# Full rows and columns for the score, gate-bias and Fourier-fold products of a two-layer hybrid backbone

## The chip, the cores and the metric

The kernel runs on one core of a Trainium2 chip. The metric is the device time of one execution in microseconds (us), the median over runs. The engines named below are TensorE (PE; its weight loads are PEld), VectorE (DVE), ScalarE (ACT), GpSimd (POOL) and SyncE (SP), which issues most DMAs.

## The reference, cut to what matters

Two layers work on 640 tokens (128 of a prompt, 512 latent ones) of width 1024. Each layer has a mixer of three branches and a gated FFN. What the change touches:

```
f = fft2(u, axes=(tokens, channels of a group of 128)).real        # branch A, 4 groups
z = (a_lr @ w_a2) + b_a                                             # branch B, gate logits, two directions
log_a = log_sigmoid(z) / 16
s = (q @ k.T) / 8;  p = softmax(s)                                  # branch C, 4 heads x 2 maps, 64 features
o = (p[map 0] - lam * p[map 1]) @ v
```

Prompt tokens see 128 keys, latent tokens 640 (128 of a cache and 512 latent ones).

## The kernel before, in words

All weight products run with operands split in a high and a low part of fp32r, three products for one (high by high, high by low, low by high; lines 391 to 393). A unit of weights is loaded, split by ScalarE (line 362) and GpSimd (line 366), and used for 640 tokens in two parts, 384 and 256 columns. TensorE runs the instructions in the order in which the program writes them. Between two groups of weight products comes a step of the other work: `slot` counts columns and calls `step`, which advances the first generator in a queue. VectorE, ScalarE and GpSimd are put in order by the scheduler, except in stretches that are written out.

**Attention (branch C).** For each layer two pairs of heads; a pair is ten tiles of 128 queries (two heads, one context tile and four latent ones each), so 40 tiles in the program, 32 of them latent. `attention` is a pipeline with ten stages, one step for each: `queries` transposes the queries of a tile into a bank of PSUM and makes their high part (ScalarE, line 1050) and their low part (GpSimd, line 1053); two steps later `maps` makes the scores; two steps after that `turn` transposes the weights, then `mix` multiplies them with the values. The 64 features of a key stand twice on the 128 partitions: in one half is the high part, in the other the low part. So the product of the high queries, whose 64 features also stand twice, takes 128 rows and yields high by high plus high by low (line 1068). The product of the low queries with the high keys takes 64 rows, the upper or lower ones for the two maps (line 1069). A latent tile has two maps of two halves of 320 keys: eight products, four of either kind in turn. A context tile has four, of 128 keys. The scores of a map take one of two PSUM buffers named `big`, which the maximum (line 1076) and the exponential (line 1079) read.

**Gates (branch B).** `gla` adds two products for each of five token tiles (line 735): the activations `aT` with 128 rows, and `ones`, 64 rows, with a table whose rows 0 and 32 hold the high and the low part of the bias. It runs once for each of two head pairs in a layer, so there are four such stretches of ten products.

**Fourier (branch A).** `fourier` takes four groups in each layer. The latent tokens are folded at their middle, which leaves one token over: its column of 128 channels is multiplied as a stationary operand with one column (line 686), and the row that results is added with a product of one row (line 709). Both are plain fp32 products, which TensorE issues twice.

**Modulation.** In layer 0 VectorE also computes the modulation (line 577), a step after so many columns of products.

Of the kernel before, what the change touches and what calls it, by code (L numbers as in the profile page):

```python
# [12 lines left out]
F32 = mybir.dt.float32  # L13
# [18 lines left out]
# the tokens in two parts, one ahead of the other  # L32
SPLIT = (slice(0, 384), slice(384, T))
STILES = ((0, 1, 2), (3, 4))
# (feature tile, part): of the last ones, the first part all before the other
# [4 lines left out]
# tiles of [128, 640]; columns of products between two steps of other work  # L40
# [6 lines left out]
def _fm(w, cols):  # L47
    """[K, M] columns as [128, K/128, 128]: one tile of output features."""
    k = w.shape[0] // P
    return w[:, cols].reshape(k, P, P).transpose(1, 0, 2)  # L50
# [66 lines left out]
def pack_mod(w):  # L117
    """The first 2048 columns of [1024, 6144] as [128, 512]: 256 of the shift and of the scale, one k tile."""
    return w[:, :2048].reshape(KT, P, 2, 4, 256).transpose(3, 0, 1, 2, 4).reshape(32, P, 512)


def pack_modt(w):
    """The columns on the partitions, as [128, 512]: 128 columns, half of the rows."""
    return w.T.reshape(48, P, 2, 512).transpose(0, 2, 1, 3).reshape(96, P, 512)


# [1 line left out]
def constants():  # L128
# [44 lines left out]
    # keys of a chunk, queries of the same half  # L173
# [8 lines left out]
# small parameters of a layer, in one [128, S] array  # L182
S_N1, S_N2, S_BM, S_GLA, S_DIF = 0, 8, 16, 64, 192
S_SIZE = 192 + 128
# and those of the differential attention
# [25 lines left out]
def pack_a2(i, l):  # L211
    """[128, 4, 128]: rows the two directions' low-rank gates, four times; [64, 4, 128]: the bias in row 0 and row 32;
    (pair, direction) columns."""
    w = i["w_gla_a2"][l]
    a, b = np.zeros((P, 4, P), w.dtype), np.zeros((64, 4, P), w.dtype)
    for pr in range(2):
        for d in range(2):
            s = slice(pr * P, pr * P + P)
            for r in range(d * 16, P, 32):
                a[r : r + 16, pr * 2 + d] = w[d][:, s]  # L220
            b[::32, pr * 2 + d] = i["b_gla_a"][l][d, s]
    return np.concatenate([a, b])


def layout(i):
# [13 lines left out]
        # [layer, pair, 2 x 64, (head, map), keys]: the 64 features twice  # L239
# [9 lines left out]
class Kernel:  # L249
    """The products of the layers' weights run on TensorE group after group; between the groups, a step at a  # L250
    time, comes the work of the branches that hangs on other engines (`side`) and of the modulation (`back`)."""
# [20 lines left out]
    # -- allocation --  # L272
# [22 lines left out]
    # -- the order of the work --  # L295
    def slot(self, cols):
        """After a product group of so many columns: steps of the other work."""
# [29 lines left out]
    def pipe(self, n, *stages):  # L327
        """Steps: stage s on item i in step i + s, the later stages first; what a stage returns is called after all of them, and so on."""
# [7 lines left out]
    # -- weights --  # L336
    def load_weight(self, halves=False):
        """The next unit in the order of use, from DRAM."""
# [10 lines left out]
    def split_weight(self, late=False):  # L349
        """The next unit in two parts."""  # L350
# [25 lines left out]
    def used(self, l, u):  # L376
        """All products of a unit are issued: its place goes to a later one."""
        del self.ws[l * N_UNITS + u]
        self.split_weight()

    def split(self, src, h, lo, eng=None):
        """src = h + lo, both of few enough bits for one pass of TensorE."""
# [3 lines left out]
    def acc3(self, ps, pairs):  # L386
        """ps = sum of (wh + wl).T @ (xh + xl) over pairs, each part in one pass."""
# [7 lines left out]
    def group(self, w, k0, nk, act, s):  # L395
        """128 output features for a part of the tokens."""
# [6 lines left out]
    def begin(self, l, us):  # L403
        """The first tokens' products of several units side by side, as their activations come."""
# [9 lines left out]
    def units(self, l, us, act, ahead=0):  # L414
        """Yields (index, ps, tokens) of the feature units us; of the first ones, the first tokens all before the others."""
# [22 lines left out]
    def proj_tm(self, l, u, act):  # L438
        """256 columns, tokens on partitions: yields (ps, token tile)."""
# [24 lines left out]
    # -- small arithmetic --  # L464
    def rsqrt(self, v, n):
        """v ** -0.5 for [128, n] in SBUF."""
# [14 lines left out]
    def load_consts(self):  # L481
# [7 lines left out]
        # with columns of zeros, so that its products fill a quarter of the array  # L489
# [4 lines left out]
    def silu(self, c, t):  # L494
        """c = c * (1 + tanh(c / 2)) / 2"""
# [22 lines left out]
    # -- modulation --  # L518
# [7 lines left out]
    def mod_first(self, raws, c, small, mod, scale1):  # L526
        """Two tiles of the first layer's first shift and scale, for both conditions: products on TensorE. Yields after
        each k; the last step turns the features to the partitions."""
# [22 lines left out]
    def mod_next(self, l, m0, m1, small, mod):  # L551
        """The columns on the partitions, tiles m0 to m1 of 128: products and their sums on VectorE."""
# [31 lines left out]
    def mod_scale(self, mod, small, gain, tile0, name):  # L584
        """gain * (1 + scale): [128, 8, 2]."""
# [7 lines left out]
    # -- norms over the model dimension --  # L593
# [9 lines left out]
    def norm_diag(self, acc, tiles):  # L603
        """1 / rms of some of the tokens, as diagonals."""
# [17 lines left out]
    def norm_rows(self, dg, ps):  # L622
        """1 / rms on all partitions."""
# [29 lines left out]
    def modulate(self, xs, acc, scale, mod, shift0, p, out):  # L653
        """h = x * rstd * scale + shift for a part of the tokens, split in two parts."""
# [7 lines left out]
    # -- branch A --  # L662
    def folds(self, u):
        """Latent tokens t and TL - t folded, since the transform's cosines are even and its sines odd."""
# [9 lines left out]
    def fourier(self, tab, us, fold, out):  # L674
# [6 lines left out]
        def channels(g):  # L681
# [4 lines left out]
            nc.tensor.matmul(pc[0:1, 256:384], u[:, TC + n2 : TC + n2 + 1], cs[:, :P], start=True, stop=True)  # L686
# [5 lines left out]
            def end():  # L692
                nc.scalar.copy(zc[:, :256], pc[:, :256])
                nc.scalar.copy(zc[0:1, 256:384], pc[0:1, 256:384])
                nc.scalar.copy(z[:, :512], pz)
# [3 lines left out]
        def tokens(g):  # L699
# [9 lines left out]
            nc.tensor.matmul(pb[:, :258], zc[0:1, 256:384], self.c("nyq", tab["fou_c"])[0:1], start=False, stop=True)  # L709
# [13 lines left out]
    # -- branch B --  # L723
    def gla(self, l, pr, aT, a2, k, q, vs, rg, outs):
        """One pair of heads. k, q: [2 heads x 64, tokens]; vs[h], rg[h]: [token, token tile, 128]."""
        nc = self.nc
        c3 = lambda ap: ap.rearrange("p (c i) -> p c i", c=NT)
        # -log_sigmoid(z) = log(1 + exp(-|z|)) + max(-z, 0)
# [23 lines left out]
        # log decay from the chunk's start (or to its end), inclusive  # L752
# [10 lines left out]
        # [keys, head, token tile, queries of the same half]  # L763
# [3 lines left out]
        def scores(kk, qq, flip=0):  # L767
            """[keys, head, 5 x 64]: the queries of the keys' half of a tile (flip: of the other half)."""
# [10 lines left out]
        # the chunks' keys decayed to their ends, and the queries from their starts  # L779
        es, dls = [], []  # L780
        # the two directions of a head, one under the other
# [31 lines left out]
        def state(d):  # L813
# [16 lines left out]
            # the state that a tile of tokens finds  # L830
# [4 lines left out]
        # attention inside a chunk, by halves of blocks; both directions in one product  # L835
# [25 lines left out]
        def place(x, y, src, copy):  # L861
            """Scores of the keys' half x and the queries' half y, to where the products with v take them."""
# [38 lines left out]
    def head_norm(self, o, gain):  # L901
        """RMS norm over the 128 of [128 tokens, token tile, 128], times gain."""
# [14 lines left out]
    def head_out(self, on, out):  # L917
        """Features to the partitions, and split."""
# [8 lines left out]
    # -- branch C --  # L927
# [34 lines left out]
    def stack(self, m, src, out):  # L962
        """The parts of [64 features twice, n]: the high one under (m = 0) or over (m = 1) the low one."""
# [4 lines left out]
    def qk_prep(self, xs, tab, out, keys=None, ko=None):  # L968
        """xs[h]: [token, token tile, 2 x 64]: QK norm, rotary; the keys transposed, a map apart, in parts."""
# [14 lines left out]
        def rotate(h):  # L984
            # a map's features twice
# [5 lines left out]
            for m in range(2):  # L991
                x, ym, wm = m4(xn)[:, :, m], m4(y[m]), m4(w)[:, 1:, m]
                # context tokens carry no position
# [28 lines left out]
    def attention(self, pr, qy, kT, kx, vd, vc, nlam, gd, outs):  # L1022
        """A pair of heads. kT[(head, map)]: the cache's and the latent tokens' keys in parts; kx [2 x 64, (head, map) x
        keys]: the context tokens'; vc [keys, head x 128]: the cache's values."""
        nc = self.nc
        qs, ps_, ws, os_ = {}, {}, {}, {}
        # a bank of PSUM that the stages of a step share: queries, outputs, a tile of the weights
# [13 lines left out]
        def queries(i):  # L1041
# [5 lines left out]
            def end():  # L1047
                q, x = self.unit("q", F32R), self.sm([P, 256], "qf", 2)
                nc.scalar.copy(x, ps[:, :256])
                nc.scalar.copy(q[:, :256], x)  # L1050
                for m in range(2):
                    r, c = slice(64 * m, 64 * m + 64), slice(m * P, (m + 1) * P)
                    nc.gpsimd.tensor_sub(q[r, 256:384], x[r, c], q[r, c].bitcast(F32))
# [4 lines left out]
        def maps(i):  # L1058
# [4 lines left out]
            for m in range(2):  # L1063
                r = slice(64 * m, 64 * m + 64)
                S = self.big().rearrange("p (x n) -> p x n", x=2)[:, :parts, :n]
                for x in range(parts):
                    k = kx[:, (2 * j + m) * P : (2 * j + m + 1) * P] if t == 0 else kT[2 * j + m][:, x * n : (x + 1) * n]
                    nc.tensor.matmul(S[:, x], q[:, m * P : (m + 1) * P], k, start=True, stop=False)  # L1068
                    nc.tensor.matmul(S[:, x], q[r, 256:384], k[r], start=False, stop=True)  # L1069
# [71 lines left out]
    # -- merge --  # L1141
    def gate(self, l, u, h):
        """tanh(gate / 2), 128 features."""
# [5 lines left out]
    def merge(self, l, u, m, act, tg, merged, first=False, parts=None):  # L1149
        """merged += (1 + tanh(gate / 2)) * y, twice the gated branch."""  # L1150
# [26 lines left out]
    def residual(self, x, ps, s, g, m):  # L1177
        """x += g * ps for a part of the tokens (in place)."""
# [5 lines left out]
    # -- one layer --  # L1184
# [11 lines left out]
    def rgate(self, l, pr, h, small, rg):  # L1196
        """silu(r) * gain"""
# [11 lines left out]
    def mixer(self, l, h, small, backs):  # L1209
        nc = self.nc  # L1210
        # Fourier
# [13 lines left out]
        # GLA  # L1225
        # 32 columns, four times; the low part of the weights in the second place. Below, the places' rows are multiplied
        # by the parts of the next weights: high and high, low and high, high and low, and the rest of the first
# [263 lines left out]
```

## Time and profile before

| | |
|---|---|
| median of 3 runs | 2443.65 us (2440.45 to 2444.65) |
| span of the profiled execution | 2444.8 us |
| TensorE busy | 2337.2 us, 96% |
| weight loads busy | 2241.7 us, 92% |
| VectorE, ScalarE, GpSimd busy | 1412.1, 881.6, 958.3 us |
| granted TensorE clock, mean | 0.985 |

The profiled execution has no time of its own beside its span; the span lies 1.15 us above the median of the runs. The ends of matmuls in a profile are modelled: two products that follow each other overlap in it, so what one costs is the distance from its start to the next one's start. A product shows as rows*columns of the array, then partitions x columns of its moving operand.

### The profile page before, as it was taken

How to read it: one execution, taken by the hardware profiler on the slowest of the kernel's cores; microseconds unless marked ns; L12 is line 12 of the kernel's file. 1: busy time of each engine (PE TensorE's matmuls, PEld its weight loads, DVE VectorE, ACT ScalarE, POOL GpSimd, SP SyncE). 2: the span in 40 equal slices, each digit the busy share in tenths (PEclk: the TensorE clock that was granted, in tenths of full speed). 3: DMA queues.
4: the chain of work that ended last, by engine and by line, in shares of the span. 5: the costliest groups of instructions: out<-in, count | busy, mean ns of one | idle time of the engine just before them, and what ended most of it. 6: DMA issues, size and time to landing. Idle time of an engine off the chain costs nothing.

```text
span 2444.8 us, 42698 instructions
## 1 busy us (share of the span) xinstructions
PE 2337.2 (96%) x17060; PEld 2241.7 (92%) x17060; DVE 1412.1 (58%) x3062; ACT 881.6 (36%) x2016; POOL 958.3 (39%) x835
## 2 busy tenths in 40 slices
PE   6989999999998999999989999999999989999999
PEld 4888898989988999999979999989899989999999
DVE  5897785665866585886464657856642462122222
ACT  3444445444243321212234554454533332122221
POOL 1343543342433443434333445524423353333332
PEclk9999999999999999999999999999999999999999
DMA  7433211111611352443331222202113122222222
GB/s 279 149 118 97 83 64 48 57 53 45 238 63 44 134 182 95 155 150 135 104 106 59 80 72 73 72 31 66 53 52 121 53 70 77 78 72 76 78 73 74
DMA packets 90181, 227.99 MB, mean 93 GB/s; under 512 B 12416, under 2 KB 20480, under 8 KB 89984
## 3 DMA queue, kind: packets, MB, share of 16 engines
q1 hardware_dynamic: 85504, 218.69, 26.2%
q10 hardware_dynamic: 4480, 6.59, 0.8%
q8 instruction: 134, 2.20, 0.4%
q14 instruction: 63, 0.52, 0.1%
HBM read 213.70 MB, written 6.82 MB: 90 GB/s over the span
## 4 chain that ended last, share of the span: by engine, by line
PE 73%; DVE 17%; issue 3%; DMA 2%; POOL 2%; ACT 1%; ACTq 0%; SPq 0%; DVEq 0%; POOLq 0%
PE main L391 20%; PE main L392 20%; PE main L393 20%; DVE junk L577 4%; PE big L412 3%; PE big L1069 2%; DVE w L1000 2%; PE big L1068 2%; PE misc L1120 2%; PE big L776 1%; DMA rawm<-in_w_modt_dram 1%; DVE rs_t L472 1%; DVE ht L650 1%; PE misc L1100 1%; DVE tg L1159 1%
## 5 line engine op out<-in xcount | busy, mean ns | idle before, releaser
L366 POOL TENSOR_TENSOR wl<-raw,wh 128x512 fp32r<-128x512 f32 x552 | 759.0, 1395 | 1167.5 <-ACT wh L362 1071.8
L362 ACT CAST wh<-raw 128x512 fp32r<-128x512 f32 x556 | 329.4, 618 | 509.0 <-PE main L392 254.6
L391 PE MATMUL main<-h2h,wh 128*128 128x256 f32 (+1 forms) x1344 | 413.3, 308 | 0.8 <-DVE tt L1315 0.8
L393 PE MATMUL main<-h2h,wl 128*128 128x256 f32 (+1 forms) x1344 | 412.9, 307 | 0.0
L392 PE MATMUL main<-h2l,wh 128*128 128x256 f32 (+1 forms) x1344 | 412.8, 307 | 0.0
L577 DVE SCALAR_TENSOR_TENSOR junk<-rawm,cond 128x512 bf16<-128x512 f32 x320 | 287.6, 899 | 40.0 <-DMA rawm<-in_w_modt_dram 35.1
L391 PE MATMUL main<-hh,wh 128*128 128x384 f32 (+1 forms) x960 | 301.3, 314 | 5.2 <-DVE rx L1201 3.5
L393 PE MATMUL main<-hh,wl 128*128 128x384 f32 (+1 forms) x960 | 296.1, 308 | 0.0
L392 PE MATMUL main<-hl,wh 128*128 128x384 f32 (+1 forms) x960 | 295.9, 308 | 0.0
L391 PEld LDWEIGHTS main<-h2h,wh 128*128 128x128 f32 x1344 | 254.6, 189 | 1.7 <-DVE tt L1315 1.3
L392 PEld LDWEIGHTS main<-h2l,wh 128*128 128x128 f32 x1344 | 254.7, 190 | 0.0
L393 PEld LDWEIGHTS main<-h2h,wl 128*128 128x128 f32 x1344 | 254.6, 189 | 0.0
L391 PE MATMUL main<-wh,hh 128*128 128x256 f32 x800 | 237.3, 297 | 0.7 <-ACT tm L461 0.7
L392 PE MATMUL main<-wl,hh 128*128 128x256 f32 x800 | 230.8, 289 | 0.0
L393 PE MATMUL main<-wh,hl 128*128 128x256 f32 x800 | 230.7, 288 | 0.0
L391 PE MATMUL main<-ah,wh 128*128 128x384 f32 (+1 forms) x704 | 219.8, 312 | 10.2 <-DVE x L1182 9.5
L392 PE MATMUL main<-al,wh 128*128 128x384 f32 (+1 forms) x704 | 218.2, 310 | 0.0
L393 PE MATMUL main<-ah,wl 128*128 128x384 f32 (+1 forms) x704 | 218.0, 310 | 0.0
L1182 DVE SCALAR_TENSOR_TENSOR x<-main,g,x 128x256 f32<-128x256 f32 (+1 forms) x192 | 78.0, 435 | 210.1 <-PE main L393 210.1
L391 PEld LDWEIGHTS main<-hh,wh 128*128 128x128 f32 x960 | 183.2, 191 | 7.2 <-DVE rx L1201 3.7
L392 PEld LDWEIGHTS main<-hl,wh 128*128 128x128 f32 x960 | 183.5, 191 | 0.0
L393 PEld LDWEIGHTS main<-hh,wl 128*128 128x128 f32 x960 | 183.3, 191 | 0.0
(281 smaller groups left out, 4774.6 us busy)
## 6 DMA issues: line engine op xcount, KB each, us to landing
raw<-in_w_dram SPq DMA_DIRECT2D x276, 512.0 KB, 3.2
rawm<-in_w_modt_dram SPq DMA_DIRECT2D x160, 256.0 KB, 4.2
rawm<-in_w_mod_dram SPq DMA_DIRECT2D x32, 256.0 KB, 5.4
x<-in_x_t_dram SPq DMA_DIRECT2D x12, 320.0 KB, 6.3
cond<-in_cond_b_dram SPq DMA_DIRECT2D x12, 256.0 KB, 5.5
qds<-qd SPq DMA_DIRECT2D x16, 160.0 KB, 2.6
x<-xd SPq DMA_DIRECT2D x8, 320.0 KB, 5.2
states<-state SPq DMA_DIRECT2D x16, 128.0 KB, 3.6
```

The lines of the kernel that those rows point to most:

```text
L362: nc.scalar.copy(h[:, c], raw)
L366: (nc.vector if late else nc.gpsimd).tensor_sub(lo[:, c], raw, h[:, c].bitcast(F32))
L391: nc.tensor.matmul(ps, wh, xh, start=(i == 0), stop=False)
L392: nc.tensor.matmul(ps, wh, xl, start=False, stop=False)
L393: nc.tensor.matmul(ps, wl, xh, start=False, stop=(i == n - 1))
L412: self.nc.tensor.matmul(self.banks[i], a, b, start=(k == 0 and n == 0), stop=(k == KT - 1 and n == 2))
L577: nc.vector.scalar_tensor_tensor(self.sm([P, 512], "junk", 1, mybir.dt.bfloat16), raw, 1.0, cond[i, k], op0=ALU.mult, op1=ALU.mult, accum_ ...
L1000: nc.vector.tensor_mul(hv(wm)[:, :, a, b], hv(x[:, 1:])[:, :, a, 1 - b], hv(sn)[:, :, a, b])
L1068: nc.tensor.matmul(S[:, x], q[:, m * P : (m + 1) * P], k, start=True, stop=False)
L1069: nc.tensor.matmul(S[:, x], q[r, 256:384], k[r], start=False, stop=True)
L1120: nc.tensor.matmul(ps, wT[:, x * P : (x + 1) * P], v, start=(x == 0), stop=(x == n - 1))
L1182: nc.vector.scalar_tensor_tensor(x[:, r], ps[:, r.start - s.start : r.stop - s.start], g[:, m, i : i + 1], x[:, r], op0=ALU.mult, op1=ALU.add)
```

## The change

The low part of the queries is made by one subtraction over 128 partitions and both maps, and its product takes 128 rows, as that of the high part does (it now adds low by low as well). The ones and the bias table are extended to 128 rows, with zeros in the table. In the Fourier branch the token left over is multiplied together with the 127 that follow it, and the row is added with 128 rows of which the table `nyq` keeps one that isn't zero.

```diff
 def pack_a2(i, l):
-    a, b = np.zeros((P, 4, P), w.dtype), np.zeros((64, 4, P), w.dtype)
+    a, b = np.zeros((P, 4, P), w.dtype), np.zeros((P, 4, P), w.dtype)
...
-            b[::32, pr * 2 + d] = i["b_gla_a"][l][d, s]
+            b[:64:32, pr * 2 + d] = i["b_gla_a"][l][d, s]
...
 # fourier, channels(g)
-            nc.tensor.matmul(pc[0:1, 256:384], u[:, TC + n2 : TC + n2 + 1], cs[:, :P], start=True, stop=True)
+            nc.tensor.matmul(pc[:, 256:384], u[:, TC + n2 : TC + n2 + P], cs[:, :P], start=True, stop=True)
...
-                nc.scalar.copy(zc[:, :256], pc[:, :256])
-                nc.scalar.copy(zc[0:1, 256:384], pc[0:1, 256:384])
+                nc.scalar.copy(zc[:, :384], pc[:, :384])
...
 # fourier, tokens(g)
-            nc.tensor.matmul(pb[:, :258], zc[0:1, 256:384], self.c("nyq", tab["fou_c"])[0:1], start=False, stop=True)
+            nc.tensor.matmul(pb[:, :258], zc[:, 256:384], self.c("nyq", tab["fou_c"]), start=False, stop=True)
...
 # attention, queries(i)
-                for m in range(2):
-                    r, c = slice(64 * m, 64 * m + 64), slice(m * P, (m + 1) * P)
-                    nc.gpsimd.tensor_sub(q[r, 256:384], x[r, c], q[r, c].bitcast(F32))
+                nc.gpsimd.tensor_sub(q[:, 256:512], x, q[:, :256].bitcast(F32))
...
 # attention, maps(i)
-                r = slice(64 * m, 64 * m + 64)
...
-                    nc.tensor.matmul(S[:, x], q[:, m * P : (m + 1) * P], k, start=True, stop=False)
-                    nc.tensor.matmul(S[:, x], q[r, 256:384], k[r], start=False, stop=True)
+                    for y in range(2):
+                        c = (2 * y + m) * P
+                        nc.tensor.matmul(S[:, x], q[:, c : c + P], k, start=(y == 0), stop=(y == 1))
...
 # mixer
-        for i, r in enumerate((slice(0, P), slice(P, P + 64))):
-            n = r.stop - r.start
-            raw, x = (self.unit("a2", t)[:n, :512] for t in (F32, F32R))
+        for i, r in enumerate((slice(0, P), slice(P, 2 * P))):
+            raw, x = (self.unit("a2", t)[:, :512] for t in (F32, F32R))
...
 # run
-            self.ones = self.cp.tile([64, P], F32R, name="ones_r")
-            nc.gpsimd.tensor_copy(self.ones, self.c("ones")[:64])
+            self.ones = self.cp.tile([P, P], F32R, name="ones_r")
+            nc.gpsimd.tensor_copy(self.ones, self.c("ones"))
```

On TensorE, at the first latent tile of the first attention, the order before is this (`q` the queries in parts, `kT` the keys of a head and map, `big` the scores; the shapes in this view leave out the rows):

```order
L393 MATMUL main_4436<-fh_868,wl_3966 128x256
L1068 MATMUL big_4460<-kT_2651,q_4349 128x320
L1069 MATMUL big_4460<-kT_2651,q_4349 128x320
L1068 MATMUL big_4460<-kT_2651,q_4349 128x320
L1069 MATMUL big_4460<-kT_2651,q_4349 128x320
L1068 MATMUL big_4465<-kT_2652,q_4349 128x320
L1069 MATMUL big_4465<-kT_2652,q_4349 128x320
L1068 MATMUL big_4465<-kT_2652,q_4349 128x320
L1069 MATMUL big_4465<-kT_2652,q_4349 128x320
L1045 MATMUL misc_4470<-const,y_4204 128x128
```

And in the changed kernel, at the same place:

```order
L393 MATMUL main_4429<-fh_868,wl_3962 128x256
L1068 MATMUL big_4453<-kT_2647,q_4344 128x320 x4
L1068 MATMUL big_4458<-kT_2648,q_4344 128x320 x4
L1045 MATMUL misc_4463<-const,y_4200 128x128
L1045 MATMUL misc_4463<-const,y_4201 128x128
```

The number of products and their neighbours are as before; the pairs of two lines have become eight of one line.

On GpSimd, at the first tiles of the same attention (`y` are rotated queries, `wl` low parts of weights, `q` the low parts of queries), the order before:

```order
L1002 COPY y_4259<-y_4259 128x4x64
L1053 TENSOR_TENSOR q_4313<-qf_4314,q_4313 64x128
L1002 COPY y_4260<-y_4260 128x4x64
L1053 TENSOR_TENSOR q_4313<-qf_4314,q_4313 64x128
L1053 TENSOR_TENSOR q_4349<-qf_4350,q_4349 64x128 x2
L366 TENSOR_TENSOR wl_4382<-raw_4152,wh_4381 128x512 x2
```

And in the changed kernel:

```order
L1002 COPY y_4255<-y_4255 128x4x64
L1052 TENSOR_TENSOR q_4309<-qf_4310,q_4309 128x256
L1002 COPY y_4256<-y_4256 128x4x64
L1052 TENSOR_TENSOR q_4344<-qf_4345,q_4344 128x256
L366 TENSOR_TENSOR wl_4376<-raw_4148,wh_4375 128x512 x2
```

The second half of the first tile's low part stood behind a copy of rotated queries; now both halves stand ahead of it. Elsewhere on GpSimd the pairs of subtractions have become single ones at their old places.

## Rows read from the trace of the kernel before

**Rows 1.** The page's first line.
```profile
span 2444.8 us, 42698 instructions
```
**Rows 2.** Windows: length, busy PE PEld DVE ACT POOL, clock, DMA share, GB/s.
```profile
132.00:136.00 4.00, 4.00 (x20) 3.87 (x21) 3.86 (x10) 0.00 (x0) 0.62 (x1) 0.57 0.59 202
140.00:150.00 10.00, 7.78 (x67) 7.58 (x65) 9.82 (x21) 8.22 (x12) 3.79 (x3) 1.00 0.00 2
400.00:420.00 20.00, 20.00 (x134) 17.22 (x133) 9.53 (x25) 11.87 (x35) 8.59 (x10) 1.00 0.18 56
1446.00:1450.00 4.00, 4.00 (x19) 3.74 (x19) 1.26 (x4) 1.72 (x7) 2.24 (x4) 0.57 0.93 313
```
**Rows 3.** Timeline of TensorE, first latent tile: start, duration, line, out<-in, rows*columns, shape.
```profile
370.77 0.28 PE L393 MATMUL main<-fh,wl 128*128 128x256 f32 x1
370.89 0.31 PE L1068 MATMUL big<-kT,q 128*128 128x320 f32 x1
371.13 0.41 PE L1069 MATMUL big<-kT,q 64*128 64x320 f32 x1
...
373.17 0.41 PE L1069 MATMUL big<-kT,q 64*128 64x320 f32 x1
373.51 0.44 PE L1045 MATMUL misc<-const,y 128*128 128x128 f32 x2
...
373.96 0.33 PE L392 MATMUL main<-hl,wh 128*128 128x384 f32 x1
374.13 0.34 PE L393 MATMUL main<-hh,wl 128*128 128x384 f32 x1
```
**Rows 4.** Source view of line 1069: durations in ns, and idle time before it.
```profile
L1069 PE MATMUL big<-kT,q x128: 406/410/413, 371.1 to 1781.5; 64*128 64x320 f32 x128
...
  issue: 19.3, 123
```
**Rows 5.** Timeline of TensorE, scores of the gated linear attention.
```profile
186.09 1.21 PE L776 MATMUL big<-eq,ek 64*64 64x64 f32 x40 [1.06 <-POOL ek L855]
```
**Rows 6.** Timeline of TensorE, first gate stretch and the product behind it.
```profile
129.15 0.28 PE L735 MATMUL big<-a,aT 128*128 128x256 f32 x1
...
132.17 0.38 PE L391 MATMUL main<-wh,hh 128*128 128x256 f32 x1
```
**Rows 7.** Timeline of TensorE, context tiles; in brackets the idle time before and its releaser.
```profile
365.65 0.22 PE L1068 MATMUL big<-kx,q 128*128 128x128 f32 x1
...
366.83 0.32 PE L1069 MATMUL big<-kx,q 64*128 64x128 f32 x1 [0.45 <-POOL q L1053]
367.09 0.44 PE L1045 MATMUL misc<-const,y 128*128 128x128 f32 x2
...
505.80 0.32 PE L1069 MATMUL big<-kx,q 64*128 64x128 f32 x1 [1.45 <-POOL q L1053]
```
**Rows 8.** Source views of lines 1053 and 366 on GpSimd: ns minimum/median/maximum.
```profile
L1053 POOL TENSOR_TENSOR q<-qf,q x80: 449/456/737, 364.3 to 1768.2; 64x128 fp32r<-64x128 f32 x80
...
L366 POOL TENSOR_TENSOR wl<-raw,wh x552: 1253/1293/1956, 21.1 to 2417.6; 128x512 fp32r<-128x512 f32 x184
```
**Rows 9.** Timeline of TensorE, a Fourier group and the start of the next.
```profile
77.73 0.60 PE L706 MATMUL big<-fou_ls,z 128*128 128x258 f32 x2
78.17 1.03 PE L708 MATMUL big<-fou_lc,z 128*128 128x258 f32 x4
...
80.70 0.49 PE L688 MATMUL misc<-fou_c,fold 128*128 128x128 f32 x2
```
**Rows 10.** Timelines of TensorE and ScalarE, the latent tile at 421.07 us.
```profile
421.07 0.39 PE L1068 MATMUL big<-kT,q 128*128 128x320 f32 x1
...
427.45 0.39 PE L1068 MATMUL big<-kT,q 128*128 128x320 f32 x1
...
425.59 0.80 ACT L1079 ACTIVATE p<-big,mx 128x640 f32<-128x640 f32 x1 [2.79 <-DVE mx L1077]
```

## The prediction

> **What bounds the kernel now.** I read the windows first. In the attention stretch TensorE is busy for all of 20 us while VectorE, ScalarE and GpSimd are busy for 9.53, 11.87 and 8.59 us, at granted clock 1.00 [rows 2]. So TensorE's own stream is the bound there, and what each product costs it is read in the timeline, from one start to the next start (the durations are modelled and overlap).
>
> The product stream has a clean pitch: a 256-column product starts 0.12 us after the one before it, a 384-column one is followed after 0.17 us. The score products don't keep that pitch. A latent tile issues eight of 320 columns, in turn with 128 rows (line 1068) and with 64 (line 1069); from 371.13 to 373.17 us six of them take 2.04 us, 0.34 us each, and the whole tile lasts from 370.89 to 373.51, 2.62 us [rows 3]. A line through 0.12 and 0.17 gives 0.147 us for 320 columns (estimate). So 0.34 is over twice what the columns need.
>
> What do the 64-row products do that the others don't? The source view says that the weight loads of line 1069 found their engine idle for 19.3 us in 123 places, with nothing to wait for but "issue" [rows 4], 0.16 us each. I read this as a change of form: the 128-row product has to be through before 64-row weights go in, and the other way round. Small products are not slow by themselves: forty 64x64 products in one form run in 1.21 us, 0.03 each [rows 5]. And the gate stretch shows the same with other operands: ten 256-column products, alternately 128 and 64 rows, last from 129.15 to 132.17 us, 0.30 each against 0.12 [rows 6].
>
> **The change part by part.** The order of each engine stays; the products keep their number and their columns. Only the rows or columns of the array that they use grow.
>
> *Scores, latent tiles.* 128 products of line 1069 at four a tile are 32 tiles [rows 4]. All eight products of a tile then have one form. 8 x 0.147 = 1.18 us in place of 2.62: 1.44 us a tile, 46.1 us in all. No row of before has a 320-column product between its like, so both ends: at the 256-column pitch (0.12) a tile takes 0.96 and the sum is 53, at the 384-column one (0.17) it takes 1.36 and the sum is 40. I take the line between, since 320 lies half way. A second estimate: the idle ahead of the 64-row loads, with as much on the way back, is 2 x 19.3 = 38.6 us, near the lower end.
>
> Here a rule of the skill is to be weighed. The Trainium skill ("TensorE: Matmul & The Clock Gate", section "LDWEIGHTS (loading the stationary operand)") says that loading weights takes as long for few rows as for 128, only columns counting, and its table of goals ("Why this matters for your kernels") that one product of few rows takes as long as a full one. By that rule alone a wider product gains nothing, and this term is 0 in place of 46. In the trace the durations agree (0.41 us for 64 rows at line 1069, as for the 128-row product beside it), but the pitch of the pair does not fit the pitch of the stream, and that is what I price.
>
> *Scores, context tiles.* Eight tiles have four 128-column products. The first lasts 365.65 to 367.09, 1.44 us, of which 0.45 is a wait for GpSimd's second half of the low part; without it 0.99 [rows 7]. In one form a 128-column product takes, by the same line, 0.07 us (bounds 0.03, the 64x64 pitch, and 0.12), a tile 0.3 to 0.4. The first tile of pair 0 saves 1.07 in both layers (the one wider subtraction now stands ahead of the copy that the second half stood behind, as the order shows), four later ones 0.6 each. The first of pair 1 waits 1.45 us for GpSimd's first half at 505.80 [rows 7]; there I count no gain, as the wider subtraction comes later. Sum 4.5 us.
>
> *GpSimd.* Two 64x128 subtractions of 456 ns become one of 128x256. Through 456 ns at 128 columns and 1293 ns at 512 [rows 8], 256 columns cost 735 ns (estimate): GpSimd saves 0.18 us a tile, off the path, but the first map's low part is ready 0.28 us later. Two steps of the pipeline cover this, except at the 505.80 wait, where it is counted above as the gain not taken (at most 0.3 us, two times).
>
> *Gate bias.* Four stretches of ten products: 3.02 us become 10 x 0.12 = 1.2; 1.82 each, 7.3 us. Moreover the granted clock is 0.57 from 132 to 136 us and 0.57 from 1446 to 1450 [rows 2], right behind two of these four stretches. 0.57 over 4 us is 3.44 us at the lower level of 1.2 GHz in place of 2.4, so 1.7 us lost in each. With the stretches dense I expect both falls gone: 3.4 us, bounds 0 and 3.4.
>
> *Fourier.* From the four products of line 708 to line 688, the ten issues with the one-row and the one-column product last from 78.17 to 80.70, 2.53 us. Two-issue products of 258 columns in one form take 0.44 (77.73 to 78.17); 708, 709, 685 and 686 would take 0.88, 0.44, 0.44 and half of it, 1.98 [rows 9]. 0.55 us in eight groups, 4.4 us. ScalarE makes one copy in place of two. The larger bias table (one more 128 KB a layer), its cast and the wider ones are done long before the gates and cost nothing.
>
> *What gives it back.* In layer 0 the modulation keeps VectorE at 9.82 of 10 us from 140 to 150, while TensorE waits (7.78) [rows 2]. What is saved ahead of that (half of the Fourier term, one gate stretch and its clock fall: 2.2 + 1.8 + 1.7 = 5.7) can only in part pass: I take off half, 3 us, bounds 0 and 5.7. In attention the faster scores push the softmax: TensorE may reuse the score buffer once the exponentials have read it. The closest tile starts at 421.07, its first exponential ends at 426.39 and the next tile's first product comes at 427.45, a slack of 1.06 us [rows 10]. The exponentials follow the scores, and VectorE and ScalarE are half idle, so the slack should mostly hold; I take off 2 us, bounds 0 and 12 (next part).
>
> Sum: 46.1 + 4.5 + 7.3 + 3.4 + 4.4 = 65.7, less 5 = 60.7. The profiled span is 2444.8 [rows 1], 1.15 above the median of the runs, 2443.65. So 2384.1 for a span, and **2383 us** for the median of runs.
>
> **The rivals.**
>
> *The scores become bound by the softmax.* If the exponential of a tile still ends 5.32 us after its first score product, however early the scores come, the next tile can't start sooner, and steps like that of 421.07 (6.38 us long) shrink by 1.06 and not by 1.44. Were all 32 so, 0.38 x 32 = 12 us come back: 2395. For it: the chain is serial over two engines. Against: both engines are about half idle [rows 2], and the chain starts at the scores.
>
> *Rows don't set the time.* The 0.34 us could belong to what these products read or write, and not to the row count; then scores and gates keep it, and only the wait of 0.45 us in two tiles and some of the Fourier term go: about 2440. This is what the Trainium skill's rule above gives. Against it speak the gate stretch and the idle ahead of the loads.
>
> *GpSimd late, and the kernel slower.* The low part of all a tile's queries now hangs on one instruction. If in each of the 40 tiles it stands behind a pair of weight subtractions (2 x 1.29 us, [rows 8]), as the wait at 505.80 suggests, TensorE loses 2.6 us a tile, 104 in all, against 66 gained: 2482. It decides from 65.7 / 40 = 1.64 us a tile. Against: before, GpSimd is free for over half of the time there, and the low part is asked for two steps later.
>
> **How the numbers follow.** My forecast with its bounds 0.83; softmax-bound 0.09; rows don't matter 0.06; GpSimd late 0.02. Range: upwards the 384-column price (+6), clock falls that stay (+3.4), all of layer 0's gain swallowed (+2.7) and part of the softmax price make 2402; downwards the 256-column price (-7), nothing given back (-5) and another fall or two of the clock less elsewhere (-3) make 2368. Faster by over 0.2% (4.9 us, about what a measurement of this kernel can tell): 0.92; within: 0.06; slower: 0.02.
>
> **What would show it.** Right: score products of one form at about 0.15 us a start, a latent tile near 1.2 us, no idle ahead of their loads; gate stretches of 1.2 us with clock 1.00 behind them; attention windows still full on TensorE. Wrong: a pitch that stays at 0.34; new waits of TensorE for an exponential or for the low part of the queries; later waits (residual norms, GLA) that grow by what was saved ahead of them.

## The result

The changed kernel takes 2386.88 us (median of 4 runs, 2380.61 to 2388.58) against 2443.28 on the same chip: a ratio of 0.9762, 95% interval 0.9746 to 0.9778. The forecast was 2383, range 2368 to 2402. The profiled execution has a span of 2383.7 us and took 2385.45. The first lines of its page answer to [rows 1] and the table before it:

```profile
span 2383.7 us, 42638 instructions
...
PE 2273.8 (95%) x17060; PEld 2233.6 (94%) x17060; DVE 1417.8 (59%) x3062; ACT 879.6 (37%) x2008; POOL 956.2 (40%) x795
```

TensorE has as many products as before and is busy for 63 us less, and the span is 61 us shorter. That is the sign of a bound engine relieved: nearly all that it saved reached the end. The timeline of TensorE at the first context tile and the first latent tile of the changed kernel, which answers to [rows 3] and [rows 7]:

```profile
360.96 0.56 PE L1068 MATMUL big<-kx,q 128*128 128x128 f32 x4
361.36 0.41 PE L1045 MATMUL misc<-const,y 128*128 128x128 f32 x2
...
365.02 0.28 PE L393 MATMUL main<-fh,wl 128*128 128x256 f32 x1
365.14 1.34 PE L1068 MATMUL big<-kT,q 128*128 128x320 f32 x8
366.31 0.38 PE L1045 MATMUL misc<-const,y 128*128 128x128 f32 x2
```

The eight products of this latent tile last from 365.14 to 366.31, 1.17 us, where 2.62 stood; the context tile 0.40 in place of 1.44. Over all 32 latent tiles the median is 1.26 in place of 2.70: most stand behind a transpose, and there the first product's pitch is 0.08 us longer in both kernels. The source view of that line says who still holds it up, and is to be read against [rows 4]:

```profile
L1068 PE MATMUL big<-kT,q x256: 302/309/418, 365.1 to 1719.4; 128*128 128x320 f32 x128
...
  POOL q L1052: 7.3, 4
  ACT p L1078: 1.2, 6
```

The row "issue" with its 19.3 us is gone. The softmax (line 1078) holds the scores for 1.2 us in all. GpSimd's 7.3 us (weight loads and products counted apart) come from the first tile of pair 1 in both layers. Three other stretches, answering to [rows 9], [rows 6] and [rows 2]: a Fourier group, the first gate stretch, and windows behind gates and in attention (columns as in [rows 2]):

```profile
78.46 1.03 PE L708 MATMUL big<-fou_lc,z 128*128 128x258 f32 x4
...
80.42 0.39 PE L689 MATMUL misc<-fou_c,fold 128*128 128x128 f32 x2
...
128.53 0.28 PE L735 MATMUL big<-a,aT 128*128 128x256 f32 x1
...
129.73 0.28 PE L391 MATMUL main<-wh,hh 128*128 128x256 f32 x1
```

```profile
128.00:132.00 4.00, 4.00 (x35) 4.00 (x35) 3.93 (x6) 0.00 (x0) 4.00 (x3) 1.00 0.41 135
1406.00:1410.00 4.00, 4.00 (x35) 4.00 (x34) 2.43 (x5) 0.42 (x1) 1.66 (x2) 1.00 0.79 265
380.00:400.00 20.00, 20.00 (x150) 19.58 (x150) 11.46 (x33) 13.82 (x40) 5.77 (x7) 1.00 0.16 53
```

Each edit does to its own products what was forecast, 1.96 us for the Fourier group and 1.20 for the gates, and the clock behind the gates is 1.00. What of it is still there later is read by setting the starts of the same product in both traces side by side (us):

```
product                                before    changed   ahead by
first context tile, layer 0            365.65    360.96     4.69
first key transpose of pair 1          471.43    453.65    17.78
norm behind the mixer, layer 0         750.14    719.17    30.97
norm behind the FFN, layer 0          1274.84   1241.68    33.16
first gate stretch of layer 1         1357.33   1322.03    35.30
first key transpose of pair 0         1545.26   1508.74    36.52
first key transpose of pair 1         1682.40   1632.77    49.63
norm behind the mixer, layer 1        1951.67   1889.27    62.40
end of the span                       2444.8    2383.7     61.1
```

The four attention stretches give 13.1, 13.2, 13.1 and 12.8, together 52.2 us. All that lies ahead of attention in layer 0 (four Fourier groups, two gate stretches) gives 4.7, in layer 1 2.1 for the Fourier groups and 1.2 for the gates. The 2.2 us gained between the two norms of layer 0 and the 1.3 lost behind the last attention belong to no part of the change; their cause stays open.

### The profile page after: what moved, and what is told of

It reads as the page before. It is cut to its first block, busy times and chain, and to the rows that moved or that the text cites. A ratio compares the mean times of both kernels' runs of the same rounds, so it can differ in the third digit from the quotient of the medians.

```text
span 2383.7 us, 42638 instructions
## 1 busy us (share of the span) xinstructions
PE 2273.8 (95%) x17060; PEld 2233.6 (94%) x17060; DVE 1417.8 (59%) x3062; ACT 879.6 (37%) x2008; POOL 956.2 (40%) x795
## 4 chain that ended last, share of the span: by engine, by line
PE 48%; DVE 7%; ACT 1%; POOL 1%; issue 1%; DMA 0%; ACTq 0%; SPq 0%; DVEq 0%; POOLq 0%
PE main L391 14%; PE main L392 14%; PE main L393 14%; PE big L412 1%; PE big L1068 1%; PE misc L1119 1%; DVE junk L577 1%; PE big L776 1%; DVE w L1000 1%; DVE ht L650 1%; DVE rs_t L472 0%; PE misc L1099 0%; DVE tg L1158 0%; DVE rs_t L473 0%; POOL ek L855 0%
```

## The experiments

The theory is the one of the prediction: a change between products of 128 and of 64 rows costs TensorE time, and removing the changes is what pays. Its rivals: a 64-row product is slow by itself; or the gain comes from clock and GpSimd. Eight kernels start from the kernel before, four from the changed one.

**One part of the change at a time.** Three kernels with the score edit, the gate edit and the Fourier edit alone, each as in the diff of the change.

*Scores alone.* 

> The kernel before with the score edit alone. By the theory that each change between 128-row and 64-row products costs time, a latent tile takes 1.2 us in place of 2.6 to 2.7 and nearly all of it reaches the end: 48 to 52 us off, about 2393. By the rival that the score gain is partly lost to the softmax or to GpSimd, and the rest of the gain came from gates and clock: 35 to 42 us off, 2402 to 2409.

Measured 2391.86 against 2444.56: ratio 0.9785 (0.9771 to 0.9800), 52.7 us off. That is a little over the first expectation, and the rival's 35 to 42 are excluded.

*Gates alone.* 

> The kernel before with the gate-bias edit alone. If dense gate stretches also spare the two falls of the clock behind them: 7.3 us for the products and 3.4 for the clock, less what layer 0 swallows, 7 to 9 us off, about 2436. If the falls only move elsewhere and later waits swallow part: 2 to 5 us off, 2439 to 2442.

Measured 2442.21, ratio 0.9989 (0.9980 to 0.9998), 2.4 us off (interval 0.5 to 4.9). The second expectation holds.

*Fourier alone.* 

> The kernel before with the Fourier edit alone. The product term says 4.4 us off. If in layer 0 the waits for the next ScalarE and VectorE results grow by what was saved, only layer 1's 2.2 us stay: about 2441.

Measured 2441.87, ratio 0.9985 (0.9976 to 0.9995), 2.7 us off: between the two numbers, nearer to the second.

The three sum up to 57.8 us; the whole change gave 56.4 by its medians and 58.2 by its repetition below. So the parts add up, and nine tenths are the scores.

**The same 64-row products, in another order.** All else is as before:

```diff
-                    nc.tensor.matmul(S[:, x], q[:, m * P : (m + 1) * P], k, start=True, stop=False)
-                    nc.tensor.matmul(S[:, x], q[r, 256:384], k[r], start=False, stop=True)
+                    nc.tensor.matmul(S[:, x], q[:, m * P : (m + 1) * P], k, start=True, stop=False)
+                    lows.append((S[:, x], q[r, 256:384], k[r]))
                 Ss.append(S)
+            for low in lows:
+                nc.tensor.matmul(*low, start=False, stop=True)
```

> The kernel before, with the same 64-row products of the low queries, but in another order: in each tile all 128-row products first, then all 64-row ones, so two changes of form a tile in place of eight. If a change costs (2.62 - 1.18) / 8 = 0.18 us, a latent tile takes 1.18 + 0.36 = 1.54 us and about 37 us come off: 2406. By the rival that a 64-row product is slow by itself (0.34 us each, whatever stands beside it), a tile takes 4 x 0.147 + 4 x 0.34 = 1.95 us at best and 2.6 at worst: 0 to 21 us off, 2422 to 2443.

Measured 2397.62, ratio 0.9805 (0.9790 to 0.9819): 46.9 us off, more than either expected. The 64-row products are all still there. That settles against "slow by itself", but the tile is too short for the theory too. Its timeline on TensorE:

```profile
367.50 0.75 PE L1068 MATMUL big<-kT,q 128*128 128x320 f32 x4
368.18 0.57 PE L1072 MATMUL big<-kT,q 64*128 64x320 f32 x4
368.68 0.33 PE L1045 MATMUL misc<-const,y 128*128 128x128 f32 x1
```

The tile lasts 1.18 us, though its form changes twice. Four 64-row products take 0.50 us, where 4 x 0.147 would be 0.59 without any change. The records of the single products show why: they start at 0.682, 0.688, 0.934 and 0.944 us of the tile, two and two. Map 0 uses the lower 64 rows of the array and map 1 the upper ones. Two further kernels test that reading.

**Both maps on the lower half.**

```diff
-                    lows.append((S[:, x], q[r, 256:384], k[r]))
+                    lows.append((S[:, x], q[:64, 256:384], k[:64]))
```

> The grouped kernel with the 64-row products of both maps on the lower half of the rows (map 1 then multiplies low queries with the other part of the keys, which leaves its right term out). In the grouped kernel the four 64-row products take 0.50 us, and their starts come in pairs 6 to 10 ns apart. If that is because two halves of the array work together, the pairs now fall apart: a start every 0.147 us, the tile 1.18 + 0.29 = 1.47 us, and 9 us more than grouped. If grouping alone made them fast, the tile stays at 1.18 us.

A single run: 2406.83 us, span 2404.8 against 2395.4 of the grouped kernel, 9.4 more. The timeline of its first latent tile:

```profile
371.74 0.75 PE L1068 MATMUL big<-kT,q 128*128 128x320 f32 x4
372.43 0.86 PE L1072 MATMUL big<-kT,q 64*128 64x320 f32 x4
373.21 0.44 PE L1045 MATMUL misc<-const,y 128*128 128x128 f32 x2
```

The tile lasts 1.47 us as expected, and the four 64-row products start at 0.681, 0.934, 1.080 and 1.230 us of it, one after the other. So the pairs were two halves of the array at work together. This tile also gives the price of a change of form without that help: 1.47 less 1.18 for eight products in one form, 0.29 us for two changes, 0.15 each. In the kernel before eight changes cost 1.44, 0.18 each. The last change also shows behind the tile: the two transposes that follow take 0.19 us in both these kernels and 0.14 in the changed one. With that a change costs 0.17 and 0.19 us.

**64 rows everywhere.**

```diff
-                    nc.tensor.matmul(S[:, x], q[:, m * P : (m + 1) * P], k, start=True, stop=False)
+                    nc.tensor.matmul(S[:, x], q[r, m * P : (m + 1) * P], k[r], start=True, stop=False)
                     nc.tensor.matmul(S[:, x], q[r, 256:384], k[r], start=False, stop=True)
```

> The kernel before with 64 rows in all eight products of a score tile (leaves out high queries by the low part of the keys): four products on the lower half of the rows, then four on the upper half, in one form. If products of different halves ran together and the form's change costs about 0.1 us, a latent tile takes at least 4 x 0.147 + 0.2 = 0.8 us where all pair up, and 1.18 + 0.2 = 1.4 us where none does; 2400 to 2390 in all. If a 64-row product were slow by itself, the tile would keep 8 x 0.34 = 2.7 us and the time 2444.

A single run: 2392.65 us, span 2390.6. Its first latent tile on TensorE:

```profile
368.35 0.43 PE L1068 MATMUL big<-kT,q 64*128 64x320 f32 x2
368.60 0.32 PE L1069 MATMUL big<-kT,q 64*128 64x320 f32 x2
368.75 0.32 PE L1068 MATMUL big<-kT,q 64*128 64x320 f32 x2
368.90 0.32 PE L1069 MATMUL big<-kT,q 64*128 64x320 f32 x2
369.15 0.33 PE L1045 MATMUL misc<-const,y 128*128 128x128 f32 x1
```

0.80 us for eight products, shorter than the 1.17 of the changed kernel, with half the rows each. Each row of the timeline is a pair of products of the two maps, though the program writes all four of map 0 ahead of those of map 1: the halves run their own streams. The whole time is not shorter than the changed kernel's. In part that is because this kernel keeps the gates and the Fourier part as before. For the rest, the 0.80 us hold only a part of the two changes of form; the other part stands beside the tile. Over all 40 tiles the products take 9.7 us less than in the changed kernel, but from the last start ahead of a tile to its first, and in the two transposes behind it, 9.3 us more go by. So this kernel comes out near the scores alone (54.5 and 52.7 us off, each against the kernel before on its chip).

**GpSimd's price doubled.**

```diff
                 nc.gpsimd.tensor_sub(q[:, 256:512], x, q[:, :256].bitcast(F32))
+                nc.gpsimd.tensor_sub(q[:, 256:512], x, q[:, :256].bitcast(F32))
```

> The changed kernel with GpSimd's subtraction of the low queries done twice (the second writes the same again), so its cost of 0.74 us doubles. By the theory that two pipeline steps hide it, only the tiles whose queries come late wait longer: the first of pair 1 in both layers, 0.7 us each, 2 us in all. By the rival that GpSimd is on the path of every tile: 40 x 0.74 = 30 us, about 2417.

A single run: 2391.62 us, span 2389.8, 6.1 more than the changed kernel's profiled 2383.7, though other runs of that one have spans up to 2387.1; so the waits say more than this difference. In layer 0 TensorE's wait for the low part is 1.4 us at the first pair, where it had none, and 2.7 at the second, in place of 1.7; in layer 1 1.4 and 2.5: 4.6 us more waiting in all, in five waits for 40 tiles. The other tiles took the doubled work without one. The rival's 30 us are excluded; my 2 us were too low, since pair 0 became late too.

**Who swallowed the gates?** In the changed kernel the waits of TensorE grew just behind the gate stretches. From 100 to 200 us (first stretch of layer 0), and from 200 to 300 us (second one):

```profile
PE main L391 <- DVE rx L1200: 5.2, 2, 3.5
...
PE main L391 <- ACT tm L461: 2.2, 2, 1.1
```

The same two rows before:

```profile
PE main L391 <- DVE rx L1201: 3.5, 1, 3.5
...
PE main L391 <- ACT tm L461: 0.7, 1, 0.7
```

To see whether VectorE's modulation is behind the first, its sums in layer 0 were cut short in the kernel before and with the gate edit:

```diff
-  self.sm([P, 512], "junk", 1, mybir.dt.bfloat16), raw, 1.0, cond[i, k], ...
+  self.sm([P, 512], "junk", 1, mybir.dt.bfloat16)[:, :w], raw[:, :w], 1.0, cond[i, k][:, :w], ...   # w = 512 if l else 8
```

> The kernel before with layer 0's modulation sums on VectorE cut from 512 to 8 columns (leaves out most of the sums; the loads stay). It is the base for the next run: what VectorE's load in layer 0 holds up by itself should show as smaller waits of TensorE from 130 to 200 us, and some 5 to 15 us off in layer 0.

> The same with the gate-bias edit. If in layer 0 VectorE's modulation swallows what the first gate stretch saves, then without that load the stretch's 1.8 us (and 1.7 more where a clock fall goes) are still there 30 us later, against the run without the edit. If something else swallows it (ScalarE's queue, or the chain behind the gates), they are gone by then here too.

Single runs: 2421.89 and 2420.56 us, spans 2419.8 and 2418.7. The base is 23 us faster than the kernel before, more than expected (15 of them are there by the first attention); TensorE's wait for VectorE's `rx` is gone in both. The waits of TensorE from 200 to 300 us, first without and then with the gate edit:

```profile
PE main L391 <- ACT tm L461: 1.1, 1, 1.1
```

```profile
PE main L391 <- ACT tm L461: 2.3, 2, 1.2
```

The wait for VectorE is its modulation's: it grows from 3.5 to 5.2 us with the edits and does not exist where the modulation is short. By starts of the same products, the gate edit alone is 3.4 us further ahead at 136 us than at 126. Of these 2.2 are gone at 140, behind a wait of 2.0 for `rx`, and the rest at 155, with a fall of the clock: it stood at 132 to 136 us before [rows 2] and stands at 152 to 155 with the gate edit (granted clock 0.50). With VectorE relieved the first stretch gains 1.6 us, all of it still there at 150, 0.7 at 160; neither of these two kernels has a fall there. But at 175 us the two cases look alike, 1.2 and 0.8 us: with the full modulation TensorE's next wait, for GpSimd (line 793), becomes shorter (3.8 to 2.3 us). So VectorE's load is a place where the gain is lost, but not what decides how much of it stays; my expectation of the last run fell in that part.

At the second stretch the wait for ScalarE's copies (line 461) grows from 1.1 to 2.3 us with VectorE relieved, from 0.7 to 2.3 with the full load and the gate edit alone, and in layer 1, where no modulation runs, from none to 1.8. The timelines of ScalarE and VectorE in the changed kernel show what stands ahead of the two copies that TensorE waits for:

```profile
227.83 0.20 ACT L949 ACTIVATE lams<-lams 128x2 f32<-128x2 f32 x1 [4.01 <-DVE lams L948]
...
228.27 0.43 ACT L461 COPY tm<-main 128x128 f32<-128x128 f32 x2 [0.24 <-ACT lams L949]
...
235.51 0.75 ACT L461 COPY tm<-main 128x128 f32<-128x128 f32 x4
...
227.18 0.29 DVE L946 TENSOR_TENSOR lamt<-dif 128x128 f32<-128x128 f32 x1 [1.65 <-DMA dif<-in_dif_dram]
```

ScalarE sits idle for 4.01 us at a small exponential (line 949). It needs a sum by VectorE, and VectorE waits there for a transfer, `dif`, that ScalarE itself issued at 223.41 us. The first copy comes right behind. From there to the second copy ScalarE runs without a break: eight passes over the gate logits (lines 740 and 741), two more (745), a table load of 1.28 us and two exponentials (747). In the kernel before the same exponential comes at 231.58 us, 4.46 us behind the start of its gate stretch; here it is 4.36. So this chain keeps its length while the stretch on TensorE gets shorter by 1.82 us. That it is the cause was read from the timelines and not tested.

**A version after the finding.** The low part of a pair's first queries on VectorE:

```diff
-                nc.gpsimd.tensor_sub(q[:, 256:512], x, q[:, :256].bitcast(F32))
+                (nc.vector if i == 0 else nc.gpsimd).tensor_sub(q[:, 256:512], x, q[:, :256].bitcast(F32))
```

> The changed kernel with the low part of a pair's first queries made by VectorE and not GpSimd. TensorE's two waits of 1.72 us for GpSimd at the first tile of pair 1 should go: 3.4 us off the changed kernel, about 2383, if VectorE is free by then; if VectorE's own queue is as late, nothing changes.

Measured 2383.36, ratio 0.9742 (0.9724 to 0.9760). TensorE's waits for the low part are now 0.4 us at pair 0 (for VectorE) and 0.5 at the second tile of pair 1 (for GpSimd), in both layers: 1.8 us in place of 3.4. To tell the two apart, both were run again on one chip:

> The changed kernel once more, on the same chip as the next run, for a comparison of the two: about 0.976 of the time before.

> The changed kernel with a pair's first low part on VectorE, again. In the trace the two waits of 1.72 us became 0.4 to 0.5: 2.4 to 2.6 us, 0.1% less than the run beside it, so about 0.975. If falls of the clock elsewhere outweigh that, the two can't be told apart.

The changed kernel: 2388.51 (2388.41 to 2388.86), ratio 0.9758 (0.9743 to 0.9773). The version: 2383.79 (2381.34 to 2388.82), ratio 0.9744 (0.9727 to 0.9761). Twice it comes out 0.14 to 0.2% lower, its slowest run is as slow as the changed kernel, and the intervals overlap: probably faster by more than the 1.6 us that the waits explain, but not settled. The rest goes with the clock: granted in the mean 0.986 in the version's five runs and 0.984 in the other's four, some 3 to 4 us over the span. No run shows that the edit brings that about.

## Why the prediction was right

*The pitch of the scores.* Right, and the largest term. A tile of 1.18 us was forecast and 1.17 measured; the line between the 256- and the 384-column pitch holds for 320. The scores gave 52.2 us in the trace and 52.7 alone, against 46.1 + 4.5 less 2 for the softmax. By starts, the products of the 40 tiles take 50 us less, waits included, close to the 50.6 ahead of that deduction: the slack of [rows 10] held, and most of the 2 us were not needed. The rest lies behind the tiles, and I had left it out: the two transposes that follow a tile take 0.06 us less, over 40 tiles 2.5 us (they no longer stand behind a change of form). That most tiles took 2.70 us before and not the 2.62 of the one I priced changes nothing, as they take 1.26 now. My second estimate counted as much idle on the way back as on the way in, 19.3 us; the loads of line 1068 show 14.1.

*The cause.* I read the idle ahead of the 64-row loads as a change of form. The grouped kernel and the one with both maps on one half bear that out: eight changes in place of two are worth 1.15 us a tile (2.62 less 1.47). The rival that rows don't set the time is out; it had the single product right (64 rows are no faster when alone), but not the change between the two. A rival that I hadn't named, that the second of two products waits because it adds to the same scores as the first, is out as well: the changed kernel has the same pairs, one right behind the other, at 0.147 us a start. What I had not seen is that 64-row products on different halves overlap.

*Gates and clock: the step that was mis-sized.* The prediction counted 7.3 us for the gate products and 3.4 for two falls of the clock, and let layer 0 take back 3 together with the Fourier part. The products did what was said and no fall stands behind the gates now; but alone they gave 2.4 us. In each layer one or both stretches are followed by a wait that grew in the changed kernel (by 1.7 us for VectorE, 1.5 and 1.9 for ScalarE). I had looked for the swallowing engine in layer 0 only, and at VectorE only. The clock gave nothing in sum: the mean granted clock is 0.985 before and 0.984 after, which over the spans is a loss of 36.7 and 38.1 us of full clock by these rounded means. The falls stand elsewhere now: two longer ones lie further behind the same two stretches, the second where one half as long stood before (columns as in [rows 2]):

```profile
148.00:155.00 7.00, 5.88 (x19) 5.88 (x20) 6.95 (x22) 1.61 (x5) 1.85 (x2) 0.51 0.66 217
1455.00:1462.00 7.00, 6.87 (x63) 6.75 (x64) 7.00 (x12) 3.28 (x6) 1.79 (x2) 0.52 0.18 42
```

*Fourier.* 1.96 us a group against 1.98 forecast; of 4.4 us 2.7 reach the end. In layer 0 the waits for the next results ahead of the gates grew by 1.6 us (at 84 us from 1.68 to 2.65, at 97 us from 0.99 to 1.66), in layer 1 2.1 of 2.2 remain.

*GpSimd.* The 128x256 subtraction takes 741 ns against 735 estimated. The wait at the first tile of pair 1 stays, 1.72 us for 1.45.

So the sum, 2384.1, came out 0.4 us from the measured span because the scores were taken 3.6 us too low (48.6 for 52.2), the terms ahead of them 4.1 too high (12.1 for 8.0), and 0.9 more came from stretches that the sum left out (2.2 gained, 1.3 lost). That these cancel is luck; the mechanism of the largest term is not. Against the median of the runs the miss is 3.9 us.

## What to carry to other kernels

Price a product by the distance to the next start, not by its duration, and compare that with the same engine's clean stream. Where products with different numbers of rows alternate, put those of one form together or give all of them the same form, before making any of them smaller. A gain on a bound engine is kept only until its next wait: look behind each stretch that gets shorter for the in-order queue that it feeds, and follow that queue back to what its head waits for.

## What the runs showed of the hardware

Two streams of 64-row products on different halves of the array ran side by side, out of the program's order: products written four places apart started 14 ns from each other, a pair of them took 0.147 us as one full product does, and eight products took 0.80 us where eight full ones take 1.17 (the part of the changes of form that lies beside the tile not counted). What stands ahead of the prediction, that TensorE runs the instructions in the order of the program, does not hold for such products. The Trainium skill ("TensorE: Matmul & The Clock Gate", section "The mechanism") tells of such overlap, and says that matmuls keep the program's order in start and end; in this trace the overlap is as it says, and the order of the starts is not kept (the ends are modelled).

A change between 128 and 64 rows cost 0.15 us where it comes twice in a tile and 0.18 where it comes eight times, 0.17 and 0.19 with what shows behind the tile. The Trainium skill ("TensorEngine Tiling (Array Packing)", section "Key Properties") says that a change of tiling mode drains TensorE, and gives no price; the trace agrees that it costs, with these numbers.
